# Gated linear attention: outputs copied out unscaled, one root for all heads, the scale at the gate; four to five places for the modulation's rows

## The chip, the core and the metric

The kernel runs on one core of a Trainium2 chip. The metric is the device time of one execution in microseconds (us); the time before is the median of three executions. The core's engines are TensorE (PE for its matmuls, PEld for its weight loads), VectorE (DVE), ScalarE (ACT), GpSimd (POOL) and SyncE (SP), which issues nearly all DMAs here.

## What is computed

One layer of a decoder trunk on 256 tokens of width 2048, in float32. The conditioning vector `c` gives six modulation segments (shift, scale and gate of two sub-layers). The first sub-layer mixes tokens in three branches; the second is a SwiGLU network. Cut to what matters here:

```python
mod = silu(c) @ w_ada + b_ada               # six segments of 2048
h = rms_norm(x, norm1_gain) * (1 + scale1) + shift1
proj = h @ w_in                             # split into the branches' columns
o_sb  = stick_breaking_attention(qa, ka, v_sb)      # 6 heads
o_dil = dilated_mixture(qb, kb, v_dil, slopes)
o_g   = gla_chunked(q_gla, k_gla, v_gla, log_a)     # 4 heads, 256 wide
o_gla = merge_heads(rms_norm(o_g, gla_out_gain)) * silu(r_gla)
y = g0 * (o_sb @ w_br_sb) + g1 * (o_dil @ w_br_dil) + g2 * (o_gla @ w_br_gla)
x = x + gate1 * (y @ w_out)                 # then the SwiGLU sub-layer
```

The line that the change rewrites is `o_gla`: each head's output is divided by its root mean square over 256 channels and multiplied by `silu(r_gla)`.

## The kernel before

**Matmuls.** Every large product is done three times in a reduced float32 form (`mm3`, lines 199 to 201): a weight piece arrives in float32, ACT casts it into a high half (`whi`, L189) and DVE subtracts it for the low half (`wlo`, L196); PE then runs high x high, high x low and low x high into one bank. These matmuls of 128x512 are nearly all of PE's work; here they are called accumulations (tile `acc`). The smaller matmuls of the branches write banks named `misc`.

**Weights.** SP fetches a weight piece of 512 KB (L160, `raw_tile`) into a room from the list `free_rooms`. There are four rooms `raw0` to `raw3`; from the fourth block of the first group on, `more_rooms` adds `A13`, `A14` and `A15`, seven in all, until the last `y_block` takes them back. A room is filled again when the DVE operation L196 on it is done. A page line that reads `A<-w_in` is a weight in one of the `A` rooms.

**Modulation rows.** The second part of the modulation (shift 2, gate 1, scale 2) is computed beside everything else on DVE: SP fetches a row of 128x1024 (`ada_rest`, L402), DVE multiplies it by a scalar and adds it to a sum (L318, `ada_mac`, here a multiply-add). `ada_segment_steps` puts one row at a time into a place of the `ring` and keeps those not yet added in `macs`; once as many wait as there are places, the oldest is added first. A multiply-add is put behind the newest split on DVE. The ring has two places, `AR0` and `AR1`; from the stage after the dilated block's norm on it has four (`AR0`, `AR1`, `KC`, `OD`, later `KD` for `OD`). `KC` also holds masks of the attentions.

**Stick-breaking attention** (L690 to L732) does six heads one after another. Per head: PE writes `z`; ACT and DVE make the two logarithms (L714 on `z`, L702 masks the diagonal, L720, L718 splits the result into two halves); PE sums them up (L723, L724, `cum`); DVE subtracts (L725), ACT takes the exponential, L702 masks again; PE multiplies by the values (L730, L731) and DVE and ACT split the output (L222). **Gated linear attention** (`gla`) builds its scores level by level (L819), ends with the scores between the two row tiles (L851, copied to `sc_cross` by L852), and then does its outputs (L858 to L874): for two row tiles and two pairs of heads, PE writes both heads of a pair into one bank (L866, L867), ACT squares each with a running sum (L869), `rsqrt` (L296 to L308: five small DVE operations and two ACT operations) makes the two roots, and ACT copies each head out, scaled (L872). The gate (L1062, L1065) multiplies by `silu(r_gla)` later, before the transposes (L1075).

**Order.** The tile framework schedules instructions on each engine by priority and dependences ahead of time; on the chip, each engine runs its list in order, and SP its list of DMAs. Accumulations of the next projection blocks fill PE's list between the small matmuls of the branches; what stands between two small matmuls is fixed by that list.

Of the kernel before, what the change touches and what calls it, by code (L numbers as in the profile page):

```python
# [10 lines left out]
F32 = mybir.dt.float32  # L11
# [3 lines left out]
ALU = mybir.AluOpType  # L15
# [52 lines left out]
def trunk(ctx: ExitStack, tc: tile.TileContext, I, out):  # L68
# [16 lines left out]
    def S(tag, shape, dtype=F32):  # L85
        return slot.tile(shape, dtype, tag=tag, name=nm(tag))

    def small(shape, dtype=F32, bufs=8):
        return sp.tile(shape, dtype, tag="tiny", name=nm("tiny"), bufs=bufs)

    def scr(shape, dtype=F32):
        return sp.tile(shape, dtype, tag="scr", name=nm("scr"))
# [78 lines left out]
    def more_rooms(*tags):  # L171
        free_rooms.extend(tags)
# [201 lines left out]
            g = vec[:, gain_row + k0 : gain_row + k0 + n]  # L374
            state["finish"] = nc.vector.scalar_tensor_tensor(dst, dst, 1.0, g, op0=ALU.add, op1=ALU.mult)

    ring = {"tags": ("AR0", "AR1"), "n": 0}

    def araw(shape, dtype=F32):
        ring["n"] += 1  # L380
        return S(ring["tags"][ring["n"] % len(ring["tags"])], shape, dtype)

    macs = []

    def mac():
        acc, j, k, raw, done = macs.pop(0)
        with tc.issue_after(state["split"].ins):
            ada_mac(acc[j], raw, k)
        if done is not None:
            after.append(done)  # L390

    def ada_segment_steps(acc, seg, done):


        for k in range(KC):
            for j in range(2):
                while len(macs) >= len(ring["tags"]):
                    mac()
                raw = araw([P, 2 * NB])
                c0 = (seg - 2) * D + j * 2 * NB  # L400
                with prio():
                    nc.sync.dma_start(raw, w_ada[k * P : (k + 1) * P, c0 : c0 + 2 * NB])  # L402
                macs.append((acc, j, k, raw, done if (k, j) == (KC - 1, 1) else None))
                yield

    def last_macs():
# [202 lines left out]
    for g in range(len(GROUPS) - 1):  # L609
        nxt = ada_group(*GROUPS[g + 1])  # L610
        steps = KC * -(-(GROUPS[g + 1][1] - GROUPS[g + 1][0]) // 4)
        done = 0
        for n, b in enumerate(orders[g]):
            while done < (steps * n // (FIN - 1) if g == 0 else steps * (n + 1) // FIN) and next(nxt, "end") != "end":
                done += 1
            if (g, n) == (0, 3):
                more_rooms("A13", "A14", "A15")
            if (g, n) == (0, 6):
                state.pop("casts_after", None)
                state.pop("macs_after", None)  # L620
            proj_block(g, b, early if (g, n) == (0, 0) else None, carry=n == 12)
        for _ in nxt:
            pass
        h_group(g + 1)
# [111 lines left out]
    def gla():  # L736
# [117 lines left out]
        def vh(h, t):  # L854
            return A[11 + h // 2][:, t, (h % 2) * T : (h % 2 + 1) * T]

        og = []
        for t in range(NT):  # L858
            o = S(f"A{9 + t}", [P, N_GLA, T])
            for h2 in range(2):  # L860
                ps = misc_bank([P, 2, T])
                ss = small([P, 2])
                for i in range(2):
                    h = 2 * h2 + i
                    if t == 1:
                        nc.tensor.matmul(ps[:, i, :], sc_cross[:, h, :], vh(h, 0), start=True, stop=False)  # L866
                    nc.tensor.matmul(ps[:, i, :], sc_same[:, t * N_GLA + h, :], vh(h, t), start=t == 0, stop=True)  # L867
                    junk = scr([P, T])
                    nc.scalar.activation(junk, ps[:, i, :], AF.Square, accum_out=ss[:, i : i + 1])  # L869
                r = rsqrt(ss, 1.0 / T, [P, 2])  # L870
                for i in range(2):
                    nc.scalar.activation(o[:, 2 * h2 + i, :], ps[:, i, :], AF.Copy, scale=r[:, i : i + 1])  # L872
            og.append(o)
        return og  # L874


    dil_q = lambda h: qg_sb[:, 1:2]
# [130 lines left out]
    state["rate"] = RATE_IN  # L1008
    proj_block(LAST, 5)
    sb_hi, sb_lo = stick_breaking()  # L1010
    og = gla()
    for b in range(6, 9):
        proj_block(LAST, b)
    qk_norm(dil_parts)

    state["rate"] = RATE_MID
    ring["tags"] = ("AR0", "AR1", "KC", "OD")

    rr = []
    groups = []  # L1020
# [25 lines left out]
    gate_block(0, 0)  # L1046
    mixture_rows(*groups)
    gate_block(0, 1)
    ring["tags"] = ("AR0", "AR1", "KC", "KD")
    gate_block(0, 2, {2: lambda: od.append(mixture(groups[0]))})  # L1050
    od = od[0]

# [5 lines left out]
    for j in range(2):  # L1058
        sg = S(f"T{1 + j}", [P, NT, NB])
        with tc.issue_after(state["last_exp"].ins):  # L1060
            nc.scalar.activation(sg, rr[j], AF.Sigmoid)
        nc.vector.tensor_mul(sg, sg, rr[j])  # L1062
        for t in range(NT):
            o = og[t].rearrange("p h d -> p (h d)")[:, j * NB : (j + 1) * NB]
            nc.vector.tensor_mul(o, o, sg[:, t, :])  # L1065
    gtag = (("A11", "A12"), ("A5", "A6"))
    for j in range(2):
        hi = S(gtag[0][j], [P, 4, T], F32R)
# [41 lines left out]
    def y_block(n):  # L1110
        y = S("T3", [P, NT, NB])
        for br, (src, kc, act) in enumerate(
# [1 line left out]
        ):  # L1114
            pss = [misc_bank([P, NB]) if br == 1 else acc_bank() for _ in range(NT)]
            if (n, br) == (3, 2):
                fewer_rooms("A13", "A14", "A15")
                more_rooms("OS0", "OS1", "OS2", "OD")
                state["ordered"] = True
                with_stages(work, pss, act, src, 0, (0, 0, 4, 6, kc), n)  # L1120
            else:
                block(pss, act, src, 0, kc, n)
# [503 lines left out]
```

## Time and profile before

| | |
|---|---|
| median of three executions | 1589.82 us (1589.38 to 1591.12) |
| profiled execution | 1590.05 us, span 1588.2 us |
| granted clock of TensorE | 1.00 |
| busy PE, DVE, ACT | 99%, 84%, 56% |
| rows of `ada_rest` into `AR` places | 58 DMAs of 512 KB, 5.0 us to landing |
| waits of DVE at L318 for them | 7.1 us in all, 5 times, longest 2.7 us |

Times in rows are microseconds from the start of the span. A row of the timeline has start, duration, engine, line, operation, output and inputs; in square brackets stands the time in which the engine was idle before it, and what released it. A matmul of 128x512 is listed with 0.39 us, while one follows another faster than that, since they are pipelined. A row of the waits has total, times and longest.

### The profile page before, as it was taken

The numbers are of one execution on the slowest core, as the hardware profiler recorded it, in microseconds if no ns is written. First come the engines' busy times: TensorE is split into PE (matmuls) and PEld (weight loads), VectorE is DVE, ScalarE is ACT, GpSimd is POOL, SyncE is SP. The second block draws the span as 40 slices with busy tenths as digits, with TensorE's granted clock in tenths as the row PEclk, the third lists the DMA queues.
The fourth block names the chain that finished last, engine by engine and source line by source line (L and its number), as shares of the span: only waits on it lengthen the run. The fifth ranks groups of instructions, "written<-read, shape, count | busy, mean of one in ns | idle before, by whom it ended". The sixth has DMA issues, their size and how long they took to land.

```text
span 1588.2 us, 20149 instructions
## 1 busy us (share of the span) xinstructions
PE 1572.1 (99%) x7207; PEld 1292.3 (81%) x7207; DVE 1334.2 (84%) x1513; ACT 893.6 (56%) x1227; POOL 5.3 (0%) x14
## 2 busy tenths in 40 slices
PE   8999999999999999999999999999999999999999
PEld 7878888778878888888888788888888888888887
DVE  6889996787878797879986899999999998877876
ACT  5654448765486444445455756666666665544543
POOL 1000000000000000000000000000000000000000
PEclk9999999999999999999999999999999999999999
DMA  9997987884776998978857665555555647797793
GB/s 334 384 354 279 334 291 252 282 271 148 237 240 211 309 325 291 327 269 298 284 162 244 192 211 199 193 191 198 197 193 209 212 141 247 257 320 254 254 323 138
DMA packets 116181, 399.24 MB, mean 251 GB/s; under 512 B 13091, under 2 KB 13897, under 8 KB 116081
## 3 DMA queue, kind: packets, MB, share of 16 engines
q1 hardware_dynamic: 115856, 397.95, 72.9%
q8 instruction: 56, 0.92, 0.2%
q14 instruction: 45, 0.36, 0.1%
q0 software_dynamic: 224, 0.01, 0.0%
HBM read 393.71 MB, written 4.19 MB: 251 GB/s over the span
## 4 chain that ended last, share of the span: by engine, by line
PE 92%; DVE 4%; DMA 2%; issue 1%; ACT 1%; POOL 0%; DVEq 0%; ACTq 0%; POOLq 0%; SPq 0%
PE acc L201 28%; PE acc L200 28%; PE acc L199 27%; DVE wlo L196 1%; PE misc L201 1%; PE misc L199 1%; PE misc L200 1%; DMA AR<-ada_rest 1%; PE misc L1106 1%; PE acc L461 1%; PE misc L819 1%; DVE ada L318 1%; PE misc L454 0%; ACT whi L189 0%; DMA H<-c 0%
## 5 line engine op out<-in xcount | busy, mean ns | idle before, releaser
L200 PE MATMUL acc<-wlo,H 128*128 128x512 f32 x1398 | 546.9, 391 | 1.1 <-DVE wlo L196 1.0
L201 PE MATMUL acc<-whi,H 128*128 128x512 f32 x1398 | 546.5, 391 | 0.4 <-DVE H L480 0.4
L199 PE MATMUL acc<-whi,H 128*128 128x512 f32 x1398 | 545.2, 392 | 0.5 <-ACT H L473 0.4
L189 ACT CAST whi<-raw 128x1024 fp32r<-128x1024 f32 (+1 forms) x302 | 310.2, 1030 | 317.5 <-PE acc L201 264.4
L196 DVE TENSOR_TENSOR wlo<-raw,whi 128x1024 fp32r<-128x1024 f32 (+1 forms) x302 | 357.6, 1194 | 128.3 <-ACT whi L189 116.4
L189 ACT CAST whi<-A 128x1024 fp32r<-128x1024 f32 (+1 forms) x240 | 248.3, 1036 | 200.3 <-PE acc L201 168.5
L196 DVE TENSOR_TENSOR wlo<-A,whi 128x1024 fp32r<-128x1024 f32 (+1 forms) x240 | 285.5, 1199 | 70.2 <-ACT whi L189 67.0
L200 PEld LDWEIGHTS acc<-wlo,H 128*128 128x128 f32 x1398 | 262.6, 188 | 57.0 <-DVE wlo L196 4.5
L199 PEld LDWEIGHTS acc<-whi,H 128*128 128x128 f32 x1398 | 262.6, 188 | 56.0 <-DVE acc L1240 1.7
L201 PEld LDWEIGHTS acc<-whi,H 128*128 128x128 f32 x1398 | 262.3, 188 | 55.5 <-DVE H L480 1.8
L199 PE MATMUL acc<-whi,A 128*128 128x512 f32 x312 | 122.4, 392 | 0.2 <-DVE acc L1240 0.2
L200 PE MATMUL acc<-wlo,A 128*128 128x512 f32 x312 | 121.6, 390 | 0.1
L201 PE MATMUL acc<-whi,A 128*128 128x512 f32 x292 | 113.9, 390 | 0.0
L199 PEld LDWEIGHTS acc<-whi,A 128*128 128x128 f32 x312 | 58.6, 188 | 13.0 <-DVE acc L1240 1.0
L200 PEld LDWEIGHTS acc<-wlo,A 128*128 128x128 f32 x312 | 58.6, 188 | 12.4 <-DVE wlo L196 0.5
L201 PEld LDWEIGHTS acc<-whi,A 128*128 128x128 f32 x292 | 54.8, 188 | 11.5
L318 DVE SCALAR_TENSOR_TENSOR ada<-AR,csil,ada 128x1024 f32<-128x1024 f32 x39 | 49.8, 1279 | 7.2 <-DMA AR<-ada_rest 7.1
L200 PE MATMUL acc<-wlo,T 128*128 128x512 f32 x120 | 46.7, 389 | 0.0
L201 PE MATMUL acc<-whi,T 128*128 128x512 f32 x120 | 46.7, 389 | 0.0
L199 PE MATMUL acc<-whi,T 128*128 128x512 f32 x120 | 46.7, 390 | 0.0
L201 PE MATMUL acc<-whi,OS 128*128 128x512 f32 x112 | 43.6, 389 | 0.0
L189 ACT CAST whi<-OS 128x1024 fp32r<-128x1024 f32 x30 | 31.7, 1056 | 21.1 <-PE acc L201 17.1
(452 smaller groups left out, 1884.8 us busy)
## 6 DMA issues: line engine op xcount, KB each, us to landing
raw<-w_in SPq DMA_DIRECT2D x118, 512.0 KB, 5.5
A<-w_in SPq DMA_DIRECT2D x85, 512.0 KB, 5.2
raw<-w_ffn_in SPq DMA_DIRECT2D x84, 512.0 KB, 4.6
raw<-w_ffn_out SPq DMA_DIRECT2D x59, 512.0 KB, 5.0
AR<-ada_rest SPq DMA_DIRECT2D x58, 512.0 KB, 5.0
A<-w_ffn_in SPq DMA_DIRECT2D x38, 512.0 KB, 4.6
H<-ada_rest SPq DMA_DIRECT2D x32, 512.0 KB, 5.0
A<-w_ffn_out SPq DMA_DIRECT2D x29, 512.0 KB, 4.8
```

The lines of the kernel that those rows point to most:

```text
L189: state["cast"] = nc.scalar.copy(hi, raw)
L196: return nc.vector.tensor_tensor(*args, **kw)
L199: nc.tensor.matmul(ps, lh, rh, start=start, stop=False, skip_group_check=seeded)
L200: nc.tensor.matmul(ps, lh, rl, start=False, stop=False, skip_group_check=seeded)
L201: state["mm"] = nc.tensor.matmul(ps, ll, rh, start=False, stop=stop, skip_group_check=seeded)
L318: nc.vector.scalar_tensor_tensor(acc, raw, c, acc, op0=ALU.mult, op1=ALU.add)
L461: state["warm"] = nc.tensor.matmul(ps, ones_r, wide, start=True, stop=True)
L819: nc.tensor.matmul(ps[:n, t * N_GLA + h, :].rearrange("p (s l) -> p s l", l=L), at(f, h, t)[:, :n], odd(at(f, h, t)), start=True, stop=True,)
L1106: nc.tensor.transpose(ps[:, i, :], src[:, i * P : (i + 1) * P], ident)
```

## The change

Three things change.

1. In `gla`, each bank with two heads is copied out by one unscaled ACT copy of 128x512, the squares then read the copy in SBUF and put their sums into eight columns of one constant tile `glas`; one `rsqrt` on all eight columns follows, and its result is copied to `glar`. At the gate, four `tensor_mul` of 128x512 become eight `scalar_tensor_tensor` of 128x256, each of which multiplies by the head's column of `glar` and by the gate.
2. The ring has four places from the start (`AR0`, `AR1`, `OD`, `A14`) and five later. `araw` passes over a place whose row has not been added yet.
3. `A14` is no longer a weight room: six rooms from the fourth block on instead of seven.

Lines behind the changed parts have numbers higher by 4 to 8: L702, L714, L718 and L720 of stick-breaking are L706, L718, L722 and L724 afterwards, L851, L866 and L867 are L855, L870 and L871. A row of the lists below has line, operation, output and inputs with their tiles' numbers, and size.

PE at the GLA outputs, from the first L866 on, before (`misc_3253` and `misc_3273` are the two pairs of heads of the first row tile, `misc_3294` and `misc_3316` those of the second, `T_698` is `sc_cross`):

```order
L866 MATMUL misc_3294<-A_184_807,T_698_3109 128x256 [waits Activation_49]
L867 MATMUL misc_3253<-A_184_807,T_697_3107 128x256 [waits Activation_49]
L867 MATMUL misc_3294<-A_184_807,T_697_3107 128x256
L866 MATMUL misc_3316<-A_194_845,T_698_3109 128x256 [waits PE_49]
L867 MATMUL misc_3316<-A_194_845,T_697_3107 128x256
L201 MATMUL acc_4031<-whi_4065,H_21_118 128x512
L199 MATMUL acc_4032<-whi_4065,H_17_114 128x512
L200 MATMUL acc_4032<-wlo_4066,H_17_114 128x512
L201 MATMUL acc_4032<-whi_4065,H_21_118 128x512
L199 MATMUL acc_4031<-whi_4065,H_17_114 128x512
L200 MATMUL acc_4031<-wlo_4066,H_17_114 128x512
L867 MATMUL misc_3273<-A_194_845,T_697_3107 128x256 [waits Activation_49]
```

The second head of each pair waits for ACT, and so accumulations stand between the heads: six before the last matmul of `misc_3273`, then 17 and 33 more before the second heads of `misc_3294` and `misc_3316`. Afterwards, from the copied scores on (`misc_3252`, `misc_3260`, `misc_3269` and `misc_3279` are the four pairs):

```order
L855 MATMUL misc_3244<-T_715_3239 128x128 x4
L871 MATMUL misc_3252<-A_184_807,T_697_3105 128x256 x2
L871 MATMUL misc_3260<-A_194_845,T_697_3105 128x256 x2
L870 MATMUL misc_3269<-A_184_807,T_698_3107 128x256
L871 MATMUL misc_3269<-A_184_807,T_697_3105 128x256
L870 MATMUL misc_3269<-A_184_807,T_698_3107 128x256
```

All twelve matmuls stand one after another, with no accumulation among them; the rest of `misc_3269` and all of `misc_3279` follow in the same way, and only the first L870 has a wait for ACT.

DVE at the second of stick-breaking's heads (head 1), from the last row before its L714 to its L718, before:

```order
L318 SCALAR_TENSOR_TENSOR ada_2554<-AR_661_2933,csil,ada_2554 128x1024
L196 TENSOR_TENSOR wlo_3010<-raw_677_3007,whi_3009 128x1024
L196 TENSOR_TENSOR wlo_3016<-raw_680_3013,whi_3015 128x1024
L714 SCALAR_TENSOR_TENSOR scr_2652<-misc_2645,scr_2648 128x384
L196 TENSOR_TENSOR wlo_3022<-raw_683_3019,whi_3021 128x512
L702 TENSOR_TENSOR scr_2652<-scr_2652,KC_2176 128x2x128
L720 SCALAR_TENSOR_TENSOR scr_2648<-misc_2645,scr_2648 128x384
L318 SCALAR_TENSOR_TENSOR ada_2554<-AR_673_2966,csil,ada_2554 128x1024
L318 SCALAR_TENSOR_TENSOR ada_2554<-AR_674_2993,csil,ada_2554 128x1024
L196 TENSOR_TENSOR wlo_3345<-A_749_3342,whi_3344 128x1024
L196 TENSOR_TENSOR wlo_3351<-A_752_3348,whi_3350 128x1024
L718 TENSOR_TENSOR T_604_2655<-scr_2652,T_604_2655 128x384
```

Three multiply-adds (L318) stand in this stretch, and two others on the rows `AR_659` and `AR_660` shortly ahead of it. Afterwards, from the last multiply-add before the head's first operation (L718 now) to the first behind L722:

```order
L318 SCALAR_TENSOR_TENSOR ada_2554<-AR_659_2901,csil,ada_2554 128x1024
L196 TENSOR_TENSOR wlo_3008<-raw_677_3005,whi_3007 128x1024
L196 TENSOR_TENSOR wlo_3014<-A_680_3011,whi_3013 128x1024
L718 SCALAR_TENSOR_TENSOR scr_2652<-misc_2645,scr_2648 128x384
L706 TENSOR_TENSOR scr_2652<-scr_2652,KC_2176 128x2x128
L196 TENSOR_TENSOR wlo_3020<-A_683_3017,whi_3019 128x512
L724 SCALAR_TENSOR_TENSOR scr_2648<-misc_2645,scr_2648 128x384
L722 TENSOR_TENSOR T_604_2655<-scr_2652,T_604_2655 128x384
L318 SCALAR_TENSOR_TENSOR ada_2554<-OD_2916,csil,ada_2554 128x1024
```

One multiply-add stands ahead of the head's operations and none among them; the rows `OD_2916` and `A_661` are added behind L722. On PE there are 49 accumulations between this head's `z` and its L723 before, 36 after, and 22 before, 20 after, between L724 and L730.

SP's list where rows for these multiply-adds are fetched, before:

```order
L402 DMA AR_646_2843<-ada_rest 128x1024
L402 DMA AR_647_2858<-ada_rest 128x1024
L160 DMA raw_680_3013<-w_in 128x1024
L160 DMA raw_683_3019<-w_in 128x512
L160 DMA A_749_3342<-w_in 128x1024
L402 DMA AR_659_2903<-ada_rest 128x1024
L402 DMA AR_660_2918<-ada_rest 128x1024
```

Rows 646 and 647 stand between weights. Afterwards, at the same place:

```order
L160 DMA raw_677_3005<-w_in 128x1024
L160 DMA A_680_3011<-w_in 128x1024
L160 DMA A_683_3017<-w_in 128x512
L406 DMA AR_659_2901<-ada_rest 128x1024
L406 DMA OD_2916<-ada_rest 128x1024
L406 DMA A_661_2931<-ada_rest 128x1024
L160 DMA raw_736_3305<-w_in 128x1024
```

Rows 646 (now in `A14`) and 647 have moved some twenty DMAs ahead, and three rows follow one another here.

The diff:

```diff
@@ -374,16 +374,20 @@
             g = vec[:, gain_row + k0 : gain_row + k0 + n]
             state["finish"] = nc.vector.scalar_tensor_tensor(dst, dst, 1.0, g, op0=ALU.add, op1=ALU.mult)
 
-    ring = {"tags": ("AR0", "AR1"), "n": 0}
+    ring = {"tags": ("AR0", "AR1", "OD", "A14"), "n": 0}
 
     def araw(shape, dtype=F32):
-        ring["n"] += 1
-        return S(ring["tags"][ring["n"] % len(ring["tags"])], shape, dtype)
+        filled = [m[5] for m in macs]
+        while True:
+            ring["n"] += 1
+            tag = ring["tags"][ring["n"] % len(ring["tags"])]
+            if tag not in filled:
+                return tag, S(tag, shape, dtype)
 
     macs = []
 
     def mac():
-        acc, j, k, raw, done = macs.pop(0)
+        acc, j, k, raw, done, _ = macs.pop(0)
         with tc.issue_after(state["split"].ins):
             ada_mac(acc[j], raw, k)
         if done is not None:
@@ -396,11 +400,11 @@
             for j in range(2):
                 while len(macs) >= len(ring["tags"]):
                     mac()
-                raw = araw([P, 2 * NB])
+                tag, raw = araw([P, 2 * NB])
                 c0 = (seg - 2) * D + j * 2 * NB
                 with prio():
                     nc.sync.dma_start(raw, w_ada[k * P : (k + 1) * P, c0 : c0 + 2 * NB])
-                macs.append((acc, j, k, raw, done if (k, j) == (KC - 1, 1) else None))
+                macs.append((acc, j, k, raw, done if (k, j) == (KC - 1, 1) else None, tag))
                 yield
 
     def last_macs():
@@ -614,7 +618,7 @@
             while done < (steps * n // (FIN - 1) if g == 0 else steps * (n + 1) // FIN) and next(nxt, "end") != "end":
                 done += 1
             if (g, n) == (0, 3):
-                more_rooms("A13", "A14", "A15")
+                more_rooms("A13", "A15")
             if (g, n) == (0, 6):
                 state.pop("casts_after", None)
                 state.pop("macs_after", None)
@@ -855,23 +859,25 @@
             return A[11 + h // 2][:, t, (h % 2) * T : (h % 2 + 1) * T]
 
         og = []
+        ss = const.tile([P, NT * N_GLA], F32, name="glas")
         for t in range(NT):
             o = S(f"A{9 + t}", [P, N_GLA, T])
             for h2 in range(2):
                 ps = misc_bank([P, 2, T])
-                ss = small([P, 2])
                 for i in range(2):
                     h = 2 * h2 + i
                     if t == 1:
                         nc.tensor.matmul(ps[:, i, :], sc_cross[:, h, :], vh(h, 0), start=True, stop=False)
                     nc.tensor.matmul(ps[:, i, :], sc_same[:, t * N_GLA + h, :], vh(h, t), start=t == 0, stop=True)
+                nc.scalar.copy(o[:, 2 * h2 : 2 * h2 + 2, :], ps)
+                for i in range(2):
                     junk = scr([P, T])
-                    nc.scalar.activation(junk, ps[:, i, :], AF.Square, accum_out=ss[:, i : i + 1])
-                r = rsqrt(ss, 1.0 / T, [P, 2])
-                for i in range(2):
-                    nc.scalar.activation(o[:, 2 * h2 + i, :], ps[:, i, :], AF.Copy, scale=r[:, i : i + 1])
+                    at_h = t * N_GLA + 2 * h2 + i
+                    nc.scalar.activation(junk, o[:, 2 * h2 + i, :], AF.Square, accum_out=ss[:, at_h : at_h + 1])
             og.append(o)
-        return og
+        r = const.tile([P, NT * N_GLA], F32, name="glar")
+        nc.vector.tensor_copy(r, rsqrt(ss, 1.0 / T, [P, NT * N_GLA]))
+        return og, r
 
 
     dil_q = lambda h: qg_sb[:, 1:2]
@@ -1008,13 +1014,13 @@
     state["rate"] = RATE_IN
     proj_block(LAST, 5)
     sb_hi, sb_lo = stick_breaking()
-    og = gla()
+    og, og_r = gla()
     for b in range(6, 9):
         proj_block(LAST, b)
     qk_norm(dil_parts)
 
     state["rate"] = RATE_MID
-    ring["tags"] = ("AR0", "AR1", "KC", "OD")
+    ring["tags"] = ("AR0", "AR1", "KC", "OD", "A14")
 
     rr = []
     groups = []
@@ -1046,7 +1052,7 @@
     gate_block(0, 0)
     mixture_rows(*groups)
     gate_block(0, 1)
-    ring["tags"] = ("AR0", "AR1", "KC", "KD")
+    ring["tags"] = ("AR0", "AR1", "KC", "KD", "A14")
     gate_block(0, 2, {2: lambda: od.append(mixture(groups[0]))})
     od = od[0]
 
@@ -1061,8 +1067,10 @@
             nc.scalar.activation(sg, rr[j], AF.Sigmoid)
         nc.vector.tensor_mul(sg, sg, rr[j])
         for t in range(NT):
-            o = og[t].rearrange("p h d -> p (h d)")[:, j * NB : (j + 1) * NB]
-            nc.vector.tensor_mul(o, o, sg[:, t, :])
+            for h in range(2 * j, 2 * j + 2):
+                o, i = og[t][:, h, :], t * N_GLA + h
+                c = slice((h % 2) * T, (h % 2 + 1) * T)
+                nc.vector.scalar_tensor_tensor(o, o, og_r[:, i : i + 1], sg[:, t, c], op0=ALU.mult, op1=ALU.mult)
     gtag = (("A11", "A12"), ("A5", "A6"))
     for j in range(2):
         hi = S(gtag[0][j], [P, 4, T], F32R)
@@ -1114,7 +1122,7 @@
         ):
             pss = [misc_bank([P, NB]) if br == 1 else acc_bank() for _ in range(NT)]
             if (n, br) == (3, 2):
-                fewer_rooms("A13", "A14", "A15")
+                fewer_rooms("A13", "A15")
                 more_rooms("OS0", "OS1", "OS2", "OD")
                 state["ordered"] = True
                 with_stages(work, pss, act, src, 0, (0, 0, 4, 6, kc), n)
```

## Prediction

> **What bounds the kernel now.** I read the page first, for the engine that fills the span, then the windows of 20 us, for the places where that engine stands idle, then the waits and the timeline at those places.
>
> ```profile
> span 1588.2 us, 20149 instructions
> PE 1572.1 (99%) x7207; PEld 1292.3 (81%) x7207; DVE 1334.2 (84%) x1513; ACT 893.6 (56%) x1227; POOL 5.3 (0%) x14
> ```
>
> TensorE is busy for 1572.1 of 1588.2 us, so everything that this change can win lies in the 16.1 us in which it stands still; the number of matmuls does not change. The windows show where those are (the first pair of columns is PE's busy time, the last three are clock, DMA share and GB/s):
>
> ```profile
> core 0: us, PE busy (x) PEld busy (x) DVE busy (x) ACT busy (x) POOL busy (x), PEclk, DMA share, GB/s
> 60.00:80.00 20.00, 20.00 (x90) 16.56 (x89) 17.04 (x17) 12.84 (x20) 0.00 (x0) 1.00 1.03 405
> 300.00:320.00 20.00, 17.73 (x81) 14.06 (x80) 18.28 (x23) 13.11 (x22) 0.00 (x0) 1.00 0.86 289
> 420.00:440.00 20.00, 19.41 (x90) 15.84 (x88) 15.14 (x25) 11.63 (x30) 0.00 (x0) 1.00 0.88 293
> 440.00:460.00 20.00, 18.11 (x80) 15.06 (x81) 14.59 (x24) 16.77 (x69) 0.00 (x0) 1.00 0.75 243
> 500.00:520.00 20.00, 19.99 (x105) 16.66 (x106) 18.19 (x29) 11.25 (x17) 0.00 (x0) 1.00 0.46 136
> ```
>
> Where the change works, PE is idle for 2.27 us in 300:320 (stick-breaking) and for 0.59 + 1.89 = 2.48 us in 420:460 (the outputs of gated linear attention, GLA). Together 4.75 us is the ceiling of the two gains. The PE timeline gives the two holes their causes:
>
> ```profile
> 309.68 0.45 PE L723 MATMUL misc<-T,T 128*128 128x384 f32 x1 [1.67 <-DVE T L718]
> 315.85 0.67 PE L730 MATMUL misc<-scr,A 128*128 128x256 f32 x2 [0.60 <-DVE scr L702]
> ```
>
> ```profile
> 438.79 0.39 PE L201 MATMUL acc<-whi,H 128*128 128x512 f32 x1
> 439.02 0.39 PE L199 MATMUL acc<-whi,H 128*128 128x512 f32 x1
> 441.89 0.70 PE L866 MATMUL misc<-A,T 128*128 128x256 f32 x2 [2.48 <-ACT scr L869]
> ```
>
> The first fence holds waits of 1.67 and 0.60 us for VectorE (1.67 + 0.60 = 2.27, the whole hole); the second ends in a wait of 2.48 us for a square on ScalarE, again the whole hole. Its first two rows also show PE's step: one accumulation every 0.23 us (439.02 - 438.79), while each is listed with 0.39 because they overlap.
>
> **Part 1: the GLA outputs.** What stands ahead of that square, on DVE and then ACT:
>
> ```profile
> 434.05 1.28 DVE L318 SCALAR_TENSOR_TENSOR ada<-AR,csil,ada 128x1024 f32<-128x1024 f32 x1 [1.65 <-DMA AR<-ada_rest]
> ...
> 436.65 0.20 ACT L301 ACTIVATE tiny<-tiny 128x2 f32<-128x2 f32 x1 [2.29 <-DVE tiny L299]
> ...
> 441.36 0.39 ACT L869 ACTIVATE scr<-misc 128x256 f32<-128x256 f32 x1
> ```
>
> A modulation row came late and held DVE for 1.65 us; behind it stood the small operations of the root; ACT waited 2.29 us for them, scaled two heads (L872), and only then could square (L869) the first half of a tile into whose other half PE had to write (L866). The change removes every link: no root stands between a matmul and its eviction, both halves are written before ACT reads them, and one copy empties both. In the order shown above, PE runs all twelve matmuls in a row. One new dependence has to be priced: the matmuls of the second row tile need `sc_cross`, which ACT copies from PSUM just before. Before, the same pieces took:
>
> ```profile
> 421.15 1.05 PE L851 MATMUL misc<-T 128*128 128x128 f32 x8
> 422.04 1.03 PE L867 MATMUL misc<-A,T 128*128 128x256 f32 x4
> ```
>
> ```profile
> 422.24 0.59 ACT L852 COPY T<-misc 128x512 f32<-128x512 f32 x1 [0.25 <-PE misc L851]
> ```
>
> The copy ends at 422.83, 1.68 us after the first L851. PE would start L866 after L851 (422.04 - 421.15 = 0.89 us) and the four L867 of the first tile (eight records; four start within 0.87 us, so 1.74), that is 2.63 us after. The copy has 0.95 us to spare: just short of one weight cast on ACT (1.05 us). So the new wait is 0 if ACT is free and at most about 1.1 us (a cast in front). I take 0.1 and a gain of **2.4 us**, bounds 1.4 and 2.5. The eight squares now read SBUF and four copies of 128x512 replace eight scaled ones, all on an engine that is 56% busy: nothing on the path.
>
> **Part 2: more places for modulation rows.** DVE at the hole of 300:320:
>
> ```profile
> 299.07 1.28 DVE L318 SCALAR_TENSOR_TENSOR ada<-AR,csil,ada 128x1024 f32<-128x1024 f32 x1 [2.69 <-DMA AR<-ada_rest]
> ...
> 302.54 0.55 DVE L714 SCALAR_TENSOR_TENSOR scr<-misc,scr 128x384 f32<-128x384 f32 x1
> 303.01 0.68 DVE L196 TENSOR_TENSOR wlo<-raw,whi 128x512 fp32r<-128x512 f32 x1
> 303.61 0.42 DVE L702 TENSOR_TENSOR scr<-scr,KC 128x256 f32<-128x256 f32 x1
> 303.95 0.55 DVE L720 SCALAR_TENSOR_TENSOR scr<-misc,scr 128x384 f32<-128x384 f32 x1
> ...
> 309.07 0.55 DVE L718 TENSOR_TENSOR T<-scr,T 128x384 fp32r<-128x384 f32 x1
> 310.69 1.28 DVE L318 SCALAR_TENSOR_TENSOR ada<-AR,csil,ada 128x1024 f32<-128x1024 f32 x1 [1.06 <-DMA AR<-ada_rest]
> ```
>
> DVE works in order, and with two places a row is fetched only when the multiply-add (L318) two rows earlier has emptied its place. Here it stood and waited for such rows, 2.69 + 1.06 = 3.75 us, of which PE felt 2.27. With four places a row is fetched before its turn. The order pieces above also show less work ahead of L718: L318 on row `661` before L714 and two more between L720 and L718, then only the one on `659`. What is late next? Head 1's L714 started at 302.54; without 2.69 us of waiting it could start at 299.85, and its chain (L714, L702, L720, L718 and one half split, as in the rows 302.54 to 303.95 and 309.07: 0.47 + 0.60 + 0.34 + 0.46 from start to start, and 0.55) takes 2.4 us: done at 302.3. PE now has 36 instead of 49 accumulations before L723, so it comes 13 x 0.227 = 3.0 us sooner: 309.68 less the wait of 1.67 is 308.0, less 3.0 is 305.0. Slack 2.7 us: that wait goes. Then L730 follows only 20 accumulations (4.5 us) and about 0.9 us of L723 and L724 (L723 is listed with 0.45, twice), at 310.4; DVE meanwhile has one small operation, two L318, two splits and L702, 0.5 + 2.4 + 2.3 + 0.4 = 5.6 us after L723's result at 305.0 + 0.5, done near 311. That is a draw, so I leave 0.3 us for it and 0.2 for the next head: 2.27 - 0.5 = **1.8 us** gained, bounds 0 (DVE's work falls due earlier and the wait forms again) and 2.3.
>
> **Part 3: six weight rooms instead of seven** until the last stage. A weight is now fetched when the room six back is free. The tightest place, by SP's queue, DVE, ACT and the DMA view of 60 to 80 us:
>
> ```profile
> 80.84 0.38 SPq L160 DMA_DIRECT2D raw<-w_in  x1
> ```
>
> ```profile
> 85.01 1.22 DVE L196 TENSOR_TENSOR wlo<-A,whi 128x1024 fp32r<-128x1024 f32 x1
> ```
>
> ```profile
> 96.86 1.05 ACT L189 CAST whi<-raw 128x1024 fp32r<-128x1024 f32 x1
> ```
>
> ```profile
> raw<-w_in SPq DMA_DIRECT2D x5, 512.0 KB, 8.9
> ```
>
> The weight issued at 80.84 would now wait for the split that ends at 86.23, 5.4 us later. With the queue as full as in 60:80 (8.9 us to landing) it lands at 95.1, still before its cast at 96.86; everywhere else before 80 us I find delays of at most 1.9 us, shorter than the 8.9 us of transfers already under way, so landings keep their times. Later the casts wait for PE and not for data:
>
> ```profile
> ACT whi L189 <- PE acc L201: 466.7, 387, 4.0
> ...
> ACT whi L189 <- DMA raw<-w_in: 10.2, 4, 7.0
> ```
>
> I take **0**, bounds 0 and 5.4 us (all of the delay reaching PE).
>
> **Part 4: the scale at the gate.** Four products of 128x512 become eight of 128x256:
>
> ```profile
> 505.19 1.28 DVE L1065 TENSOR_TENSOR A<-A,T 128x512 f32<-128x512 f32 x2
> ...
> 509.11 0.48 DVE L1082 SCALAR_TENSOR_TENSOR A<-misc,vec,A 128x256 fp32r<-128x256 f32 x1
> ```
>
> 8 x 0.48 - 2 x 1.28 = 1.3 us more on DVE. In 500:520 DVE is idle for 1.81 us and PE for 0.01, so the idle time covers it: 0, bounds 0 and 1.3. The Trainium skill ("Advanced Engine Details and Errata", TRN2 Errata, The Read-Write Bubble) speaks against this edit: it says that VectorE pays an unhidden access time at every instruction, and advises tiles of 512 or 1024 elements. The row agrees (0.48 us for half of what takes 0.64); by that rule the sum would be the same unless the extra falls on the path, which is a rival below.
>
> **Sum.** Against the profiled execution (1590.05 us, of which 1.85 lie around the span): -2.4 - 1.8 + 0 + 0 = -4.2, so 1585.85. It ran 0.23 above the median of 1589.82, so against the median 1585.6; I say **1585.7**. Orders after 520 us change too, but PE has no large hole there: +-0.5.
>
> **Rivals.**
> - *The wait in stick-breaking forms again.* For it: fewer accumulations stand before L723, and DVE was busy 18.28 of 20 us. Against: 3.75 us of DVE waiting go. It includes the case that the added places do nothing, because rows queue on SP behind weights and still land late. Only 2.4 are gained: 1587.4.
> - *The GLA hole is refilled* by a DVE held up on modulation rows, so that a split comes late and PE waits for it instead. Of the six L318 there one waits 1.65 us; if that still delays a split past its use, only 1.8 are gained: 1588.0.
> - *The gate falls on the path*: 1.3 us back, 1586.9. For it: DVE's idle time in 500:520 exceeds the added work by only 0.5 us.
> - *Slower: the rooms starve the load-bound stage.* Up to 120 us the DMA share is near 1 (1.03 in 60:80). It decides when a room comes free more than 8.9 us after the issue that it holds up: the queue then runs dry and six rooms move 1/7 less per lap. From 60 to 120 us that is 60/7 = 8.6 us: 1589.8 - 4.2 + 8.6 = 1594.2. Against: the worst delay that I find is 5.4.
>
> **How the numbers follow.** Forecast 0.55; wait forms again 0.15; GLA hole refilled 0.10; gate 0.11; starving 0.09. About 0.2% (3.2 us, so below 1586.6 or above 1593.0) is what a measurement can tell from no change. The forecast case reaches from 1584.5 to 1586.6 and is nearly all in "faster", with a little of the gate's; starving, with part of its delay only, stays within: faster 0.56, same 0.37, slower 0.07. The range from 1584.2 to 1590.2 leaves out the starving case and a tenth on the other side.
>
> **What would show it.** Right: in 420:460 PE busy for 40 us less at most 0.2, with no L866 among its waits; in 300:320 an idle time of about 0.5; at DVE's L318 in 285 to 320 no wait for ada_rest over 0.5 us. Part 3: PE busy 20.00 in the windows from 40 to 80 us as before, and no wait of PE for a split (wlo L196) in the first 120 us that was not there. Part 4: 500:520 still at 19.9 or more. Wrong: such a wait, there or in 420 to 460.

## The result and the profile after

On the chip on which it was first compared, the changed kernel took 1586.4 us (median, 1585.31 to 1586.65) and the kernel before 1590.95 us (1589.38 to 1592.46): ratio 0.9972, 95% interval 0.9961 to 0.9982. On a second chip the ratio was 0.9964 (0.9950 to 0.9977). The forecast was 1585.7 us, from 1589.82 us before.

The windows of the changed kernel at the places that the prediction named (PE's busy time comes first, then PEld, DVE, ACT and POOL, the clock, the DMA share and GB/s):

```profile
0.00:20.00 20.00, 15.74 (x61) 12.58 (x62) 8.02 (x17) 9.65 (x24) 4.28 (x13) 1.00 0.84 300
60.00:80.00 20.00, 20.00 (x89) 16.52 (x89) 16.96 (x18) 12.98 (x20) 0.00 (x0) 1.00 1.03 405
80.00:100.00 20.00, 18.61 (x85) 14.81 (x84) 16.07 (x22) 14.81 (x23) 0.00 (x0) 1.00 0.90 334
300.00:320.00 20.00, 20.00 (x92) 16.24 (x91) 19.61 (x27) 15.20 (x26) 0.00 (x0) 1.00 0.94 330
420.00:440.00 20.00, 20.00 (x105) 16.72 (x104) 17.72 (x22) 14.21 (x35) 0.00 (x0) 1.00 0.82 263
440.00:460.00 20.00, 19.86 (x95) 16.17 (x94) 17.43 (x25) 15.84 (x59) 0.00 (x0) 1.00 0.95 323
500.00:520.00 20.00, 20.00 (x98) 16.45 (x97) 19.43 (x29) 11.63 (x17) 0.00 (x0) 1.00 0.68 210
```

Both holes are gone: 300:320 went from 2.27 us of idle time to 0.00, 420:460 from 2.48 to 0.14. In the same view, 0:20 is a new one (4.26 us idle against 2.99 before), which did not return in the next execution (2.83, below).

The windows count idle time only up to the modelled end of the last matmul, which is later than the next one could have started. For what each place was worth in full, I took the start of the same accumulation in both traces and subtracted. Both have the same 6390 accumulations, in the same order but for 40 of them between 774 and 815 us. The rows are at places where PE had also done the same number of other matmuls in both:

```
accumulation   before     after   difference   what lies between it and the row above
           0    33.07     33.62        +0.55   the first DMA, norm 1
        1120   299.92    300.19        +0.27   the loading stage, six rooms
        1207   326.79    324.50        -2.29   stick-breaking's head 1
        1680   477.58    472.75        -4.83   its later heads and the GLA outputs
        1920   542.95    537.79        -5.16   the dilated block and the gate
        2920   774.39    769.45        -4.94   the stage behind the gate
        3120   823.58    819.50        -4.08   DVE's full stretch
        6320  1568.66   1564.42        -4.24   the last stage
```

Stick-breaking gave 2.6 us, its later heads and the GLA outputs 2.5, the dilated block 0.3; then 1.1 were lost between 540 and 824 us, 0.9 of them behind 774, a place that the prediction had left at +-0.5. DVE and PE there, in the changed kernel:

```profile
803.13 1.22 DVE L196 TENSOR_TENSOR wlo<-H,whi 128x1024 fp32r<-128x1024 f32 x1
804.27 1.28 DVE L318 SCALAR_TENSOR_TENSOR ada<-KC,csil,ada 128x1024 f32<-128x1024 f32 x1
...
808.93 1.27 DVE L318 SCALAR_TENSOR_TENSOR ada<-KD,csil,ada 128x1024 f32<-128x1024 f32 x1
```

```profile
805.70 0.74 PE L365 MATMUL misc<-ident,ada 128*128 128x128 f32 x5 [0.69 <-DVE ada L318]
```

DVE is busy without a pause here, and two multiply-adds stand in it. PE cannot transpose the finished sum (L365) before the first of them is done and waits 0.69 us. Before the change DVE had done the last multiply-add well ahead of this stretch:

```profile
791.46 1.27 DVE L318 SCALAR_TENSOR_TENSOR ada<-AR,csil,ada 128x1024 f32<-128x1024 f32 x1
```

With five places, the last two rows of the segment are held back longer; in DVE's list their multiply-adds moved from behind the 273rd split (L196) to behind the 285th and the 287th.

### The profile page after: what moved, and what is told of

The parts are those of the page before. It is cut to its first block, busy times and chain, and to the rows that moved or that the text cites. A ratio compares the mean times of both kernels' runs of the same rounds, so it can differ in the third digit from the quotient of the medians.

```text
span 1584.4 us, 20142 instructions
## 1 busy us (share of the span) xinstructions
PE 1570.6 (99%) x7207; PEld 1292.1 (82%) x7207; DVE 1334.1 (84%) x1503; ACT 892.4 (56%) x1217; POOL 5.3 (0%) x14
## 4 chain that ended last, share of the span: by engine, by line
PE 92%; DVE 4%; ACT 1%; DMA 1%; issue 1%; POOL 0%; SPq 0%; DVEq 0%; ACTq 0%; POOLq 0%
PE acc L201 28%; PE acc L200 28%; PE acc L199 28%; DVE wlo L196 2%; PE misc L199 1%; PE misc L201 1%; PE misc L200 1%; PE misc L1114 1%; PE acc L465 1%; PE misc L823 1%; ACT whi L189 1%; PE misc L458 0%; DMA H<-c 0%; DVE ada L318 0%; PE misc L365 0%
## 5 line engine op out<-in xcount | busy, mean ns | idle before, releaser
L189 ACT CAST whi<-raw 128x1024 fp32r<-128x1024 f32 (+1 forms) x326 | 335.1, 1031 | 344.2 <-PE acc L201 298.2
L196 DVE TENSOR_TENSOR wlo<-raw,whi 128x1024 fp32r<-128x1024 f32 (+1 forms) x326 | 386.5, 1196 | 118.1 <-ACT whi L189 112.1
L196 DVE TENSOR_TENSOR wlo<-A,whi 128x1024 fp32r<-128x1024 f32 x216 | 257.1, 1199 | 80.6 <-ACT whi L189 78.0
L189 ACT CAST whi<-A 128x1024 fp32r<-128x1024 f32 x216 | 223.4, 1036 | 176.5 <-PE acc L201 152.2
L318 DVE SCALAR_TENSOR_TENSOR ada<-H,csil,ada 128x1024 f32<-128x1024 f32 x30 | 37.4, 1280 | 0.0
```

Of the source, the lines that this page charges most:

```text
L189: state["cast"] = nc.scalar.copy(hi, raw)
L196: return nc.vector.tensor_tensor(*args, **kw)
L318: nc.vector.scalar_tensor_tensor(acc, raw, c, acc, op0=ALU.mult, op1=ALU.add)
```

## The experiments

Each time is a median; ratios are to the kernel before on the same chip, with their 95% intervals (a ratio is not the quotient of the two medians). The runs came in three groups, each on one chip, where the kernel before took 1590.59, 1590.98 and 1589.56 us. PE's idle time is from the windows of the profiled execution, added up over the stretch; each column holds every wait of PE there, whatever it waited for.

| run | us | ratio | idle 280 to 420 | idle 420 to 460 | idle 780 to 830 |
|---|---|---|---|---|---|
| before (first profile) | 1590.59 | 1 | 2.27 | 2.48 | 0.37 |
| e1_gla: part 1 alone | 1587.15 | 0.9975 (0.9965 to 0.9984) | 2.13 | 0.16 | 0.37 |
| e6_both: both heads first | 1588.89 | 0.9990 (0.9980 to 0.9999) | 2.28 | 0.61 | 0.37 |
| e2_ring: ring and rooms alone | 1586.08 | 0.9973 (0.9961 to 0.9984) | 0.03 | 0.00 | 0.96 |
| e3_rooms: six rooms alone | 1588.15 | 0.9985 (0.9976 to 0.9993) | 2.93 | 0.00 | 0.37 |
| after_again: the changed kernel | 1586.05 | 0.9964 (0.9950 to 0.9977) | 0.01 | 0.15 | 0.92 |
| e4_tail4: four places at the end | 1584.89 | 0.9955 (0.9943 to 0.9968) | 0.12 | 0.15 | 0.40 |
| e5_lag2: at most two rows waiting | 1586.13 | 0.9964 (0.9951 to 0.9976) | 0.10 | 0.12 | 0.90 |
| e7_three: three places, seven rooms | 1585.01 | 0.9955 (0.9943 to 0.9968) | 0.07 | 0.16 | 0.36 |
| e7_again: the same | 1584.76 | 0.9967 (0.9956 to 0.9979) | 0.06 | 0.16 | 0.37 |
| e9_three_nogla: that without part 1 | 1585.52 | 0.9974 (0.9965 to 0.9983) | 0.07 | 0.63 | 0.38 |
| e8_ring_tail: e4_tail4 without part 1 | 1585.46 | 0.9972 (0.9963 to 0.9981) | 0.16 | 0.88 | 0.37 |

**Part 1 alone.** The kernel before with the new `gla` and the new gate.

```diff
-    og = gla()
+    og, og_r = gla()
...
-            nc.vector.tensor_mul(o, o, sg[:, t, :])
+                nc.vector.scalar_tensor_tensor(o, o, og_r[:, i : i + 1], sg[:, t, c], op0=ALU.mult, op1=ALU.mult)
```

> The kernel before with part 1 alone (unscaled copies, one root, the scale at the gate); two places in the ring and seven rooms as before, and the lists around stick-breaking and at 800 us as before. Theory: only the hole at the GLA outputs goes, so PE is idle 0.1 to 0.3 us in 420 to 460 (2.48 before) and still 2.3 in 300 to 320: 2.4 us faster than before, ratio 0.9985. Rival (the late row was the cause and the root only its messenger): PE waits for a split there instead, less than 1 us gained, ratio over 0.9994.

The hole at the outputs went (0.16 us left) and the one in stick-breaking stayed (2.13). The theory held in place; the time fell by 3.4 us where 2.4 were expected. The profiled execution is 2.3 us shorter than that of before (1587.75 against 1590.05), so no hole accounts for the extra microsecond between the medians.

**Both heads first.** One line of the kernel before is split into two loops; everything else of part 1 is left out.

```diff
                     nc.tensor.matmul(ps[:, i, :], sc_same[:, t * N_GLA + h, :], vh(h, t), start=t == 0, stop=True)
+                for i in range(2):
                     junk = scr([P, T])
```

> The kernel before with one line moved: both heads of a pair are multiplied into their bank before ACT squares the first one; the four roots, the scaled copies, the gate, the ring and the rooms are as before. Theory A (the roots between matmul and eviction hold PE up): 1.5 us or more of the hole at the GLA outputs stays, less than 1 us gained. Theory B (the shared bank is the link: PE could not write the second half until ACT had read the first): the hole goes as in the run with the whole part 1, 2.4 us gained, ratio 0.9985.

PE and ACT in this run (PE's last pair, then ACT on the same bank):

```profile
426.36 0.59 PE L866 MATMUL misc<-A,T 128*128 128x256 f32 x2
426.79 0.59 PE L867 MATMUL misc<-A,T 128*128 128x256 f32 x2
458.61 0.77 PE L682 MATMUL misc<-ident,A 128*128 128x128 f32 x4 [0.61 <-DVE A L670]
```

```profile
435.57 0.20 ACT L301 ACTIVATE tiny<-tiny 128x2 f32<-128x2 f32 x1 [2.09 <-DVE tiny L299]
436.38 0.39 ACT L870 ACTIVATE scr<-misc 128x256 f32<-128x256 f32 x1
```

The roots are as late as before (ACT waits 2.09 us for DVE), but PE had finished all twelve matmuls at 427.4 and did not notice. So the link was the shared bank, as theory B says, and not the root as such. What is left, 0.61 us, is a wait of the next block's transposes (L682) for their norm on DVE (L670), which worked without a pause from 447.97 us until then. The gain in time, 1.7 us, is below the 2.4 expected, with an interval that nearly reaches 1.

**Ring and rooms alone.** The changed kernel with the old `gla` and gate.

```diff
-    og, og_r = gla()
+    og = gla()
```

> The changed kernel with part 1 undone: more places in the ring and six rooms alone. Theory (the parts are independent): 2.3 to 2.7 us gained in stick-breaking, about 1.1 lost at 795 to 810 us, the GLA hole of about 2.5 stays: 1.5 us faster than before, ratio 0.9991. Rival (with rows fetched earlier DVE is on time for the roots too): the GLA hole shrinks below 1 us and the gain is 3 us or more, ratio 0.998.

My theory fell: this run is as fast as the whole change. The GLA hole is gone without part 1, in the size that the rival named. PE and ACT at the last pair, to be read against the 441.36 square and the 441.89 matmul of before:

```profile
424.45 1.05 PE L855 MATMUL misc<-T 128*128 128x128 f32 x8
...
442.47 0.59 PE L870 MATMUL misc<-A,T 128*128 128x256 f32 x2
```

```profile
441.50 0.38 ACT L873 ACTIVATE scr<-misc 128x256 f32<-128x256 f32 x1
```

```profile
426.65 1.28 DVE L318 SCALAR_TENSOR_TENSOR ada<-KC,csil,ada 128x1024 f32<-128x1024 f32 x1 [0.95 <-DMA KC<-ada_rest]
```

PE reaches the pair's second head 18.0 us after the first L855 (442.47 - 424.45). Before, it would have reached it after 18.1 (439.02 + 0.23 - 421.15). But the square that it needs starts 17.05 us after L855, where it started 20.2 us after L851 before (441.36 - 421.15). DVE waits 0.95 us for a row in this stretch instead of 2.23 (0.58 + 1.65), which is 1.3 of these 3.2 us; the rest comes with the new order of the lists. PE is spared by 442.47 - 441.88 = 0.6 us.

**Six rooms alone.** The ring has two places.

```diff
-                more_rooms("A13", "A14", "A15")
+                more_rooms("A13", "A15")
```

> The kernel before with six rooms instead of seven and nothing else; two places in the ring. The scheduler's lists change in stick-breaking (the multiply-adds now stand behind L718, and 35 instead of 49 accumulations before head 1's L723). Theory (the ring's places take the stick-breaking hole away): DVE still waits for rows, 1.5 us or more of the 2.27 stays, the time is within 1 us of before. Rival 1 (the new order in the lists does it, whatever the ring): the hole falls below 0.7 us, 2 us faster. Rival 2 (six rooms starve the casts): PE idle more than 1 us longer in 40 to 120 us, slower by 2 us or more.

The waits of PE in stick-breaking in this run, on the timeline:

```profile
337.86 0.44 PE L723 MATMUL misc<-T,T 128*128 128x384 f32 x1 [0.55 <-DVE T L718]
360.91 0.44 PE L723 MATMUL misc<-T,T 128*128 128x384 f32 x1 [1.43 <-ACT T L717]
366.72 0.67 PE L730 MATMUL misc<-scr,A 128*128 128x256 f32 x2 [0.95 <-DVE scr L702]
```

and DVE's waits for rows, over the whole run:

```profile
DVE ada L318 <- DMA AR<-ada_rest: 6.1, 7, 2.3
```

Rival 2 is out: the windows from 40 to 100 us are idle for 1.40 us as before (1.39), so the seventh room was worth nothing there. Rival 1 is out for stick-breaking: the new order in the lists only moved the stick-breaking waits to later heads (2.93 us together), since rows still came late with two places: the largest, 1.43 us for ACT, stands behind a wait of DVE for a row of 2.28 us. That part of the theory held. Its time did not: 2.4 us faster, because the GLA hole vanished here too, with a margin of 0.3 us (the square ended at 442.75, PE came at 443.06). DVE still waited 0.74 and 0.47 us for rows at the GLA outputs, 1.0 us less than before, while the square came 4.9 us sooner behind L851 (442.39 - 427.04 = 15.35 us). So most of it is the new order of the lists, with the ring as before.

**The changed kernel again**, and its tail with four places.

> The changed kernel once more, to stand beside the next three on the same chip: 4.5 us faster than before, ratio 0.997. If the 0.36 us that PE starts later and the 0.44 us at the end are of the execution and not of the kernel, they differ here.

0:20 is idle for 2.83 us in this execution, and accumulation 1120 starts at 299.93, as before the change (299.92): the late start of the first profile was of that execution. The end did not differ. From the start of the last accumulation to the end of the span there are 4.66 us in both profiles of the changed kernel and 4.22 before, so these 0.44 us come with the kernel, and about 0.3 us more lie outside the span in its executions. With four places at the end (`e4_tail4`) both are gone (4.23 us); why is open.

```diff
-    ring["tags"] = ("AR0", "AR1", "KC", "KD", "A14")
+    ring["tags"] = ("AR0", "AR1", "KC", "KD")
```

> The changed kernel with four places instead of five in the ring's last setting, so that the last multiply-adds of scale 2 stand at the same splits as before the change (the last at split 273 instead of 285 and 287). Theory (the fifth place let the last two multiply-adds slip into the stretch where DVE is full, and the transposes L365 wait for them): PE's wait of 0.85 us at L365 near 804 us goes, 0.7 to 1.1 us faster than the changed kernel. Rival (DVE is simply full there and PE comes 5 us earlier): PE waits for something else, the same time within 0.3 us.

PE and DVE at L365 with four places:

```profile
810.33 0.63 PE L365 MATMUL misc<-ident,ada 128*128 128x128 f32 x4 [0.30 <-DVE A L222]
```

```profile
786.44 1.28 DVE L318 SCALAR_TENSOR_TENSOR ada<-AR,csil,ada 128x1024 f32<-128x1024 f32 x1
```

and PE at L365 before the change:

```profile
815.37 0.63 PE L365 MATMUL misc<-ident,ada 128*128 128x128 f32 x4 [0.27 <-DVE A L222]
```

The last multiply-add is back at 786, L365 waits 0.30 us for something else, as before the change, and the time is 1.16 us below the changed kernel on the same chip. The theory held: the fifth place costs 1.1 us in DVE's full stretch (281.73 us from accumulation 1920 to 3120 in `after_again`, 280.60 here). That the medians differ by about as much is in part luck: this execution was 0.6 us behind at accumulation 1920, and won 0.7 us after the last one.

**At most two rows waiting**, with four places.

```diff
-                while len(macs) >= len(ring["tags"]):
+                while len(macs) >= min(ring.get("lag", 2), len(ring["tags"])):
```

> The changed kernel with four places in the ring, but at most two rows waiting for their multiply-add up to the stage behind the dilated block's norm, as before the change. Theory (the places let rows be fetched early): DVE has no wait for a row over 0.5 us in 285 to 350, PE's idle time there stays under 0.5 us, the time is that of the changed kernel within 0.7 us. Rival (it is the later multiply-adds that clear DVE's list): PE's waits at L723 and L730 come back, 1.5 us or more, and the time is 1.5 us above the changed kernel.

Idle 0.10 us from 280 to 420, no wait of DVE for a row there, and the same time as the changed kernel. As in `e3_rooms`, no multiply-add stands among head 1's four DVE operations, and there PE was idle for 2.93 us with rows that came late: the earlier fetch is what counts, not the later multiply-add.

**Three places first, seven rooms.** `A14` stays a weight room.

```diff
-    ring = {"tags": ("AR0", "AR1", "OD", "A14"), "n": 0}
+    ring = {"tags": ("AR0", "AR1", "OD"), "n": 0}
...
-    ring["tags"] = ("AR0", "AR1", "KC", "OD", "A14")
+    ring["tags"] = ("AR0", "AR1", "KC", "OD")
...
-    ring["tags"] = ("AR0", "AR1", "KC", "KD", "A14")
+    ring["tags"] = ("AR0", "AR1", "KC", "KD")
```

> The changed kernel with three places in the first ring (AR0, AR1, OD) and four later, A14 being a weight room again (seven rooms). Theory (one place more is enough, and the tail's loss goes): stick-breaking's holes are under 0.7 us together, no wait at L365 near 805 us, 0.5 to 1 us faster than the changed kernel. Rival (four places are needed): 1 us or more of PE's idle time comes back in 285 to 350, as slow as the changed kernel or slower.

> The changed kernel with three places first, four later and seven rooms once more, to stand beside the next two on the same chip: about 1585.0, ratio 0.9955 to 0.997.

One place more than before was enough for stick-breaking (0.07 and 0.06 us left), and nothing is lost at the tail: 1585.01 us, 1.04 below the changed kernel on the same chip. This version and `e4_tail4` beat both kernels; the two cannot be told apart.

**Is part 1 needed beside the ring?** The last version without part 1, and `e4_tail4` without it.

> The same three places and seven rooms without part 1, that is the kernel before with one more place (OD) in the first ring. PE's list at the GLA outputs reads 6, 17 and 36 accumulations before the three late matmuls (6, 17, 33 before the change; 8, 24, 23 and 6, 18, 22 in the two runs where the hole was gone without part 1). Theory (the hole hangs on where the list puts the last pair, and part 1 takes that dependence away): 1 to 2.5 us of the hole are back in 420 to 460, and it is 1 to 2.4 us slower than the run with part 1. Rival (rows fetched earlier keep DVE on time for the roots wherever the pairs stand): idle under 0.5 us there, the same time within 0.5 us.

> Four places first, five in the middle, four at the end, six rooms, without part 1. Theory (with this order the hole is gone without part 1, so part 1 adds nothing here): within 0.5 us of the run with four places at the end and part 1, 1584.9, no idle time over 0.3 us in 420 to 460. Rival (part 1 is worth its own time elsewhere, fewer operations on ACT and DVE): 1 us or more slower.

The first came out 0.8 us above the run with part 1 on the same chip (1585.52 against 1584.76; the ranges, 1585.38 to 1586.29 and 1584.03 to 1584.94, do not meet), between the theories. But of its 0.63 us of idle time only 0.02 stand at the GLA outputs:

```profile
437.79 0.70 PE L870 MATMUL misc<-A,T 128*128 128x256 f32 x2
456.78 0.44 PE L686 MATMUL misc<-ident,A 128*128 128x128 f32 x2 [0.61 <-DVE A L674]
```

The 0.61 are the wait of the next block's transposes that was left in `e6_both` too. At the last pair PE was not held, though DVE waited longer for rows than before the change (0.18 + 1.64 + 1.02 us; 2.23 before):

```profile
431.32 1.28 DVE L318 SCALAR_TENSOR_TENSOR ada<-AR,csil,ada 128x1024 f32<-128x1024 f32 x1 [1.64 <-DMA AR<-ada_rest]
435.04 1.28 DVE L318 SCALAR_TENSOR_TENSOR ada<-KC,csil,ada 128x1024 f32<-128x1024 f32 x1 [1.02 <-DMA KC<-ada_rest]
```

```profile
437.24 0.40 ACT L873 ACTIVATE scr<-misc 128x256 f32<-128x256 f32 x1
439.32 0.84 ACT L876 ACTIVATE A<-misc,tiny 128x256 f32<-128x256 f32 x2 [0.66 <-DVE tiny L307]
```

ACT's list has the square ahead of the scaled copies that wait for the root; before the change it stood behind them (440.63 and 441.36). So here the order of the lists alone took PE out of the chain.

The second run was on another chip than its partner, so only its trace is used:

```profile
432.01 0.70 PE L871 MATMUL misc<-A,T 128*128 128x256 f32 x2 [0.76 <-ACT scr L873]
```

```profile
429.27 1.28 DVE L318 SCALAR_TENSOR_TENSOR ada<-KC,csil,ada 128x1024 f32<-128x1024 f32 x1 [2.75 <-DMA KC<-ada_rest]
```

Up to here PE, DVE and ACT run the same instructions in the same order as in `e2_ring`, which differs only in the ring's last setting. There the row came 0.95 us late and PE did not wait; here it came 2.75 us late, the root and the square behind it were late as well, and PE waited 0.76 us. So with one and the same order the hole hangs on when a row lands. Without part 1 PE waited 2.48, 0.00, 0.00, 0.02 and 0.88 us at the GLA outputs (before, `e2_ring`, `e3_rooms`, `e9_three_nogla`, `e8_ring_tail`); with both heads written first it did not wait there in any of eight profiles. That is what part 1 is worth beside the ring: in these runs the place no longer hangs on the order or on the rows. Of the 0.8 us between `e7_again` and `e9_three_nogla`, the transposes' wait makes 0.45 (0.16 against 0.61); the rest was not traced.

## Why the prediction was right, point by point

**What bounds the kernel**: right. PE's idle time fell at the two places named, and the time with it.

**Part 1**: right in size where it stands alone (2.48 to 0.16 us idle; 2.4 had been forecast), and PE's new wait for `sc_cross` did not come: ACT copied it at 426.60, and PE came at 428.13.

```profile
426.40 1.89 PE L871 MATMUL misc<-A,T 128*128 128x256 f32 x8
428.13 0.59 PE L870 MATMUL misc<-A,T 128*128 128x256 f32 x2
```

```profile
426.60 0.59 ACT L856 COPY T<-misc 128x512 f32<-128x512 f32 x1 [1.10 <-PE misc L855]
```

What the prediction did not see: parts 2 and 3 close the same hole. The chain that it quoted rested on two things, a row that came late and a list in which the square stands behind the root; one room less or one place more changes the lists, and when the row lands differed by 1.8 us even under the same lists. The gains were added as if the parts were independent. They are not: part 1 alone gained 3.4 us, ring and rooms alone 4.5, the whole 4.5 (first chip) and 4.9 (second). The sum came out because each hole was counted once, not because each part had its own.

**Part 2**: right in cause, short in size: 1.8 forecast, 2.6 by the starts of accumulations, 2.27 of 2.27 by idle time. The working hid an error. I let PE run from `z` to L723 over 36 accumulations instead of 49, but the L723 that waited was the second of the head (it reads the low half that L718 makes), and 11 more stood ahead of it before, 2 after: 38 instead of 60, so PE came 5.0 us sooner and not 3.0. The changed kernel's rows:

```profile
303.45 0.35 PE L727 MATMUL misc<-T,T 128*128 128x384 f32 x1
...
309.01 0.59 PE L734 MATMUL misc<-scr,A 128*128 128x256 f32 x2
```

```profile
302.62 0.55 DVE L722 TENSOR_TENSOR T<-scr,T 128x384 fp32r<-128x384 f32 x1
...
308.21 0.42 DVE L706 TENSOR_TENSOR scr<-scr,KC 128x256 f32<-128x256 f32 x1
```

DVE was done at 303.17 and PE came at 303.45: the slack was 0.3 us where I had 2.7. The second wait, which I called a draw, went the good way by 0.4 us (308.63 against 309.01). DVE's wait for rows in the `AR` places, 7.1 us before, is no longer among the waits of the changed kernel (1.4 us for rows in `KC` are); `e3_rooms`, which left the ring alone, still had 6.1.

**Part 3**: right for the whole change, 0. The loading stage shows the same idle time, 20.00 busy in 60:80 and 1.39 idle in 80:100, and so did `e3_rooms`. The rival of starving rooms did not come. But the prediction priced the rooms by that stage alone: one room less also reorders the lists behind it, and by itself made the kernel 2.4 us faster.

**Part 4**: right. A gate product took 477 ns where 0.48 us was assumed, and PE's idle time in 460:520 went from 0.34 to 0.27 us, with none in 500:520:

```profile
L1073 DVE SCALAR_TENSOR_TENSOR A<-A,glar,T 128x256 f32<-128x256 f32 x8 | 3.4, 477 | 0.0
```

The Trainium skill's advice of larger tiles ("Advanced Engine Details and Errata", TRN2 Errata, The Read-Write Bubble) agrees with the row's size: 477 ns for half of a product that took 682 ns before. It had no price here, since DVE had idle time: the products ran from 497.90 to 504.74 us, and DVE was still idle for 3.74 us in 480:500 and for 0.57 in 500:520.

**After 520 us**: the +-0.5 was too narrow. The lists had shown the two multiply-adds behind the 285th and 287th split; that they would stand ahead of L365 in a stretch where DVE has no pause was there to be read, and it cost 1.1 us. Together with the underestimate of part 2 it is why the sum came out so close: -2.6 - 2.5 - 0.3 + 1.1 = -4.3, where -4.2 had been forecast. That is luck, since two errors cancel. So is part of the time: the two profiled executions differ by only 3.4 us (1590.05 and 1586.63), as the changed one started late and ended late, and the medians by 4.55 us, as the kernel before ran at 1590.95 us beside the changed one and not at the 1589.82 that the forecast started from.

## What to carry to other kernels

Two parts that cut the same chain of waits do not add: before summing, ask of each hole which parts could close it alone, and run each part alone. Where an engine works in order and a transfer can hold it up, one more place to fetch into can be worth as much as rearranging its work (4.0 us in `e9_three_nogla`, 3.4 in `e1_gla`, each against the kernel before on its chip), but a further place can also let the last work slip later: look at what stands behind the last one. A change that looks free, as one room less, can still reorder the lists and open or close a wait elsewhere: run it alone. When a matmul must write into a bank that another engine is still reading, write all of the bank first.

## What the runs showed of the hardware

Under the same lists a row of 512 KB kept DVE waiting for 2.75 us in one execution and for 0.95 in another, and PE stood still for 0.76 us at the GLA outputs in the first and not at all in the second. The kernel before spread from 1588.02 to 1593.31 us over 26 runs in the first group; the changed kernel from 1585.31 to 1586.65 over 8, and 1586.00 to 1586.54 over 5. The version with both heads first, whose DVE still waits for rows, spread from 1587.15 to 1592.86 over 11. But `e1_gla`, whose DVE waits 6.3 us for rows in `AR` places, spread only from 1585.87 to 1587.75 over 9, and `e3_rooms`, with 6.1 us of such waits, from 1587.33 to 1589.69 over 11. So waits for transfers do not by themselves go with a wide spread; what varies from run to run was not traced. ACT's square of 128x256 took 412 ns from SBUF and had taken 382 ns from PSUM, after and before:

```profile
L876 ACT ACTIVATE scr<-A 128x256 f32<-128x256 f32 x8 | 3.3, 412 | 0.1
```

```profile
L869 ACT ACTIVATE scr<-misc 128x256 f32<-128x256 f32 x8 | 3.1, 382 | 3.7 <-PE misc L867 3.7
```
